# First-norm row factors multiplied in behind the products for the first pair of blocks, and the second pair's gates one block product later

## The chip, the cores and the metric

The kernel runs on one NeuronCore of one Trainium2 chip. Its time is device microseconds of one execution. TensorE (PE) multiplies matrices into PSUM; VectorE (DVE), ScalarE (ACT) and GpSimd (POOL) work on SBUF and, the first two, on PSUM; SyncE (SP) and GpSimd issue most DMA transfers. Each engine takes its instructions in order.

## What is computed

One layer of a decoder trunk on x, 2048 rows of 1024 fp32 values:

```python
h = rmsnorm(x, norm_mix_g)                   # x * rsqrt(mean(x*x) + eps) * g
u = h @ w_in                                 # 3*512 + 2*1024 columns
gate_b, gate_c, v, x_r, g = split(u)
y_conv = gate_b * causal_dwconv(gate_c * v, conv_w)       # 3 taps
xr = causal_dwconv(x_r, rnn_conv_w) + rnn_conv_b          # 4 taps
r, i = sigmoid(blockdiag(xr, w_a) + b_a), sigmoid(blockdiag(xr, w_x) + b_x)
log_a = -8 * r * softplus(-lru_lambda); a = exp(log_a)
s[t] = a[t] * s[t-1] + sqrt(-expm1(2*log_a)) * (i * xr)[t]
y_rnn = s * gelu(g)
x = x + concat[rmsnorm(y_conv), rmsnorm(y_rnn)] @ w_out
x = x + square(relu(rmsnorm(x) @ w_mlp_in)) @ w_mlp_out
out = rmsnorm(x)
```

The first line has a factor for each row (1 over its root mean square) and a gain for each of the 1024 columns. A row factor commutes with the product by w_in, a gain does not.

## The kernel before

**Tiles.** Channels lie on the 128 partitions and rows on the free axis, so h is read transposed, from a transposed x in HBM (x_t, tiles xT). The 2048 rows are four blocks of 512, worked on in two pairs. A weight or an h value is kept as two rounded parts, hi and lo, and a product of 128 x 128 by 512 is three matmuls, hi by hi, hi by lo, lo by hi. round_off (L165 to L167) makes the parts: ScalarE copies to hi, VectorE subtracts for lo.

**First pair, mixers_plain.** The columns of w_in are worked in groups of 256, in the order x0 g0 x1 g1 x2 g2 x3 g3 c0 v0 c1 v1 b0 b1. A group on one block is 48 matmuls into one PSUM tile of two banks (ps_x, ps_g and so on; start_x for x0 on block 0), and there are four such tiles. For each pair of x and g, the two units u0 and u1 (class Lru, 128 channels each) do the recurrence: conv makes xr and its parts xr_hi and xr_lo; gate sends 12 matmuls into two PSUM tiles called psri, followed by four sigmoids that make r and gi; scan makes the coefficients, with tanh, exponential and square root on ScalarE, and runs the recurrence; out multiplies by gelu(g) into gi and adds the square to acc. u1's gate comes behind the next pair's x on block 0.

**Weights.** A unit of w_in is two tiles of 512 KB called raw, split into w_hi and w_lo. Some halves are spilled to HBM (d_ws) for the second pair. keep_sums makes four sums of raw weights (weight_sums, L638 to L641) and stores them (d_wk), also for the second pair. Tiles come from pools with a fixed number of slots, so a tile waits for the last user of its slot.

**The start.** The rows of block 0 are loaded in two halves (x), squared on ScalarE and summed; norm_rows makes the row factors; spread makes diagonals of them (L361) and multiplies by ones on TensorE (bc, L368), so that a factor stands on all partitions; scale_rows (L373) multiplies xT by it and the gain; the result is split to h_hi and h_lo. WARM matmuls of ones by ones (L385, L388) fill TensorE ahead. Block 1 goes the same way in prepare_second, between g0 and x0 on it, with its rows in xq.

**Second pair, mixers_blocks.** Two blocks and two halves of the contraction make 2 x 2 products, done with seven block products of 24 matmuls each (L778), in the order 1, 2, 6, 5, 7, 3, 4. The gates, scans and outs of the group before are placed behind the block products by the table STEPS: step 0 is u0's gate and u1's conv, 1 u0's scan, 2 u1's gate and u0's out, 3 u1's scan, 4 u1's out. The first group has a row of its own.

**Order.** Outside parts that stand as written (manual_schedule, around x0 on block 0), a scheduler of the framework moves instructions on each engine within what data, slots and issue_after (hold these behind a named instruction) allow. So the order in the code is not quite that on the engines.

Of the kernel before, what the change touches and what calls it, by code (L numbers as in the profile page):

```python
# [14 lines left out]
P = 128  # L15
SEQ = 2048
D = 1024
KD = D // P
# [11 lines left out]
WARM = 6  # L30
# [9 lines left out]
STEPS = {1: (0,), 2: (1,), 6: (2,), 5: (3,), 7: (4,)}  # L40
# [19 lines left out]
def block_kernel(  # L60
# [60 lines left out]
    def load(dst, src):  # L121
        nc.sync.dma_start(dst, src)
# [65 lines left out]
    def split_unit(u):  # L188
        if u >= len(units) or u in splits:
            return  # L190
        load_unit(u)
        rs = raws.pop(u)
        n = units[u][3]
        pairs = [split_new(r, wtile, "w") for r in rs]
# [80 lines left out]
    def load_xt_part(b, th):  # L275
        for q in range(2):
            r = temp("xT", (P, 4, 256))
            c0 = b * TB + th * 256
            src = x_t[q * 512 : q * 512 + 512, c0 : c0 + 256]
            xtt[b, q, th] = r  # L280
            load(r, src.rearrange("(k p) s -> p k s", p=P))

# [18 lines left out]
    load_x(0, (0,))  # L301
    load(prm, params)
    load_xt_part(0, 0)
    load_x(0, (1,))
    load_unit(0)
    load_xt_part(0, 1)
# [36 lines left out]
    def squares(b, ts):  # L343
        s2 = [small("s2_%d" % i)[:, : len(ts)] for i in range(2)]
        for i in range(2):
            for k, t in enumerate(ts):
                xv = x_half(b, t, i)
                nc.scalar.activation(xv, xv, AF.Square, accum_out=s2[i][:, k : k + 1])
        return s2

# [23 lines left out]

    start_x = psum("start_x")
    with tc.manual_schedule(
        engines={nc.scalar.engine, nc.vector.engine, nc.tensor.engine}
    ):
        h0 = (
            hp.tile([P, KD, TB], F32R, tag="h", name="h_hi"),  # L380
            hp.tile([P, KD, TB], F32R, tag="h", name="h_lo"),
        )
        rs = norm_rows(squares(0, (0, 1)), 2)
        for _ in range(WARM):
            nc.tensor.matmul(start_x[:, 0, :P], ones, ones, start=True, stop=True)  # L385
        bc = spread(rs, 2)
        for _ in range(WARM):
            nc.tensor.matmul(start_x[:, 0, :P], ones, ones, start=True, stop=True)  # L388
        sq = squares(0, (2, 3))

        def first(th, q, ns=range(3)):
            for n in ns:
                a, b = ((0, 0), (0, 1), (1, 0))[n]
                for j in range(2):
                    for k in range(4):
                        nc.tensor.matmul(
                            start_x[:, j, 256 * th : 256 * th + 256],
                            w_first[a][q][:, k, j * P : (j + 1) * P],
                            h0[b][:, 4 * q + k, 256 * th : 256 * th + 256],
                            start=q == 0 and n == 0 and k == 0,  # L400
                            stop=q == 1 and n == 2 and k == 3,
                        )

        for th in range(2):
            sl = slice(256 * th, 256 * th + 256)
            r = [xtt[0, q, th] for q in range(2)]
            hi = [h0[0][:, 4 * q : 4 * q + 4, sl] for q in range(2)]
            lo = [h0[1][:, 4 * q : 4 * q + 4, sl] for q in range(2)]
            scale_rows(r[0], 0, bc, 4)
            nc.scalar.copy(hi[0], r[0])  # L410
            scale_rows(r[1], 4, bc, 4)
            if th == 0:
                rs = norm_rows(sq, 2)
                w_first = take("x0", ahead=0)
                first(0, 0, (0,))
                bc = spread(rs, 2)
            nc.scalar.copy(hi[1], r[1])
            for q in range(2):
                V.tensor_tensor(lo[q], r[q], hi[q].bitcast(F32), SUB)
            first(th, 0, range(1 - th, 3))  # L420
            first(th, 1)
        split_unit(1)
# [12 lines left out]
    V.tensor_scalar(l_neg, lam, -1.0, 0.0, MUL, MAX)  # L435
    V.scalar_tensor_tensor(l_abs, l_neg, 2.0, lam, MUL, ADD)
    nc.scalar.activation(l_u, l_abs, AF.Exp, scale=-1.0)
    V.tensor_scalar(l_d, l_u, 2.0, None, ADD)
    V.reciprocal(l_d, l_d)
    V.tensor_mul(l_w, l_u, l_d)  # L440
    V.tensor_mul(l_w2, l_w, l_w)
    V.tensor_scalar(l_s, l_w2, 2.0 / 15, 2.0 / 13, MUL, ADD)
    for n in (11, 9, 7, 5, 3, 1):
        V.tensor_mul(l_s, l_s, l_w2)
        V.tensor_scalar(l_s, l_s, 2.0 / n, None, ADD)
    V.tensor_mul(l_s, l_s, l_w)
    V.tensor_add(l_s, l_s, l_neg)
    V.tensor_scalar(sp4, l_s, -4.0, None, MUL)
    V.tensor_scalar(sp8, l_s, -8.0, None, MUL)
# [8 lines left out]

    class Rows:

        def __init__(self, b, rs):
            self.b = b
            self.rs = rs
            self.s2 = [small("s2_%d" % i) for i in range(2)]

        def part(self, n):
            th, dh = n // 2, n % 2
            r = temp("xq")
            load(r, x_rows(self.b, th, dh))
            for k in range(2):  # L470
                c = 2 * th + k
                nc.scalar.activation(
                    r[:, k], r[:, k], AF.Square, accum_out=self.s2[dh][:, c : c + 1]
                )

        def factors(self):
            norm_rows(self.s2, NT, self.rs)

        def spread(self, bc):
            nc.scalar.copy(bc, spread(self.rs, NT))  # L480
# [172 lines left out]
    def mixers_plain(h):  # L653
# [3 lines left out]
        nxt = [Rows(2 + k, rs_next[:, k, :]) for k in range(2)]  # L657

# [6 lines left out]
        for pr in range(4):  # L665
            u0, u1 = Lru(2 * pr), Lru(2 * pr + 1)
            xin = new_xin(pr)
            g = wide("g")

            def drain_x(blk, ps):  # L670
                nc.scalar.copy(block(xin, blk, 3), ps)
# [24 lines left out]
            u1.conv(xin)  # L696
            both("g%d" % pr, drain_g, (1,), wg)
            u0.gate(gw)
            u0.scan()
            p0, p1, gp_ = u0, u1, g  # L700
            keep_sums(pr)
            for n in range(2):
                nxt[pr // 2].part(2 * (pr % 2) + n)
            if pr % 2:
                nxt[pr // 2].factors()
        us = []
        for pr in range(2):
            gc = wide("gc")
            cv = new_cv(pr)
            wc = both("c%d" % pr, lambda blk, ps: nc.scalar.copy(block(gc, blk), ps), (0,))  # L710
            if pr == 0:
                p1.gate(gw)
            both("c%d" % pr, lambda blk, ps: nc.scalar.copy(block(gc, blk), ps), (1,), wc)
# [10 lines left out]
            us.append(conv_short(pr, cv))  # L724
            keep_sums(4 + pr)
# [140 lines left out]
    def mixers_blocks(H, more):  # L866
# [7 lines left out]
        for n in range(-FETCHW, len(seq)):  # L874
# [327 lines left out]
    def prepare_second():  # L1202
        rows = Rows(1, small("rs_x"))
        for n in range(4):
            rows.part(n)
        load_xt(1)
        rows.factors()
        bc = temp("bcs", (P, TB))
        rows.spread(bc)
        his, los = [], []  # L1210
        for q in range(4):
            r = xtt[1, q]
            scale_rows(r, 2 * q, bc, 2)
            hi, lo = split_new(r, temp, "h1")
            his.append(hi)
            los.append(lo)
        h[1] = lambda k: (his[k // 2][:, k % 2, :], los[k // 2][:, k % 2, :])

# [224 lines left out]
```

## Time and profile before

| | us |
|---|---|
| median of 3 runs | 2199.39 (2197.33 to 2199.86) |
| the profiled execution | 2200.14 |
| its span, first to last instruction | 2198.3 |
| TensorE busy in the span | 2138.3 |
| VectorE busy | 1481.1 |
| ScalarE busy | 994.7 |

About 1.9 us of an execution lie outside the span. A row of the view by windows gives the busy time of each engine in one stretch, with its instructions in brackets, and at the end the clock that TensorE was granted (1.00 is full), the share of time that the DMA engines were busy, and GB/s. A row of the view of waits names an operation, what it waited for, the total, the number of times and the longest. TensorE's matmuls overlap, so the distance of two starts and not the length is what one costs.

### The profile page before, as it was taken

What the parts mean: (1) busy time and instruction counts of PE and PEld (TensorE: products, weight loads), DVE (VectorE), ACT (ScalarE), POOL (GpSimd) and SP (SyncE); (2) the same over time, 40 slices, a digit from 0 to 9 for tenths busy, and PEclk for the clock granted to TensorE, in tenths of its full rate; (3) what the DMA queues carried; (4) which work ended last, traced back from release to release, by engine and by line L of the source; (5) the groups of instructions that cost most, each with busy time, mean ns of one, the idle gap of its engine ahead of it and who ended that gap; (6) DMA issues with size and microseconds to landing.
All of it is one profiled execution on the core that took longest, in us unless ns stands there. A gap on an engine that the chain in (4) does not pass through costs nothing.

```text
span 2198.3 us, 25153 instructions
## 1 busy us (share of the span) xinstructions
PE 2138.3 (97%) x9514; PEld 1755.2 (80%) x9514; DVE 1481.1 (67%) x1739; ACT 994.7 (45%) x1238; POOL 165.9 (8%) x288
## 2 busy tenths in 40 slices
PE   6999999999999999999998999999999999999998
PEld 5777787888887888888887777878878888888886
DVE  6688864669877786577764778466887565654456
ACT  5688712435323335454535786244533333433333
POOL 0111110000111110000131121000000000000000
PEclk9999999999999999999999999999999999999999
DMA  9645565431786789799673554655134444876431
GB/s 335 215 165 187 210 223 183 156 138 53 283 300 248 292 310 403 273 385 341 236 255 118 167 182 154 224 177 182 49 124 183 150 166 153 320 290 234 163 141 77
DMA packets 179593, 464.14 MB, mean 211 GB/s; under 512 B 15376, under 2 KB 64528, under 8 KB 179472
## 3 DMA queue, kind: packets, MB, share of 16 engines
q1 hardware_dynamic: 146416, 346.12, 43.9%
q0 software_dynamic: 30176, 106.97, 13.1%
q10 hardware_dynamic: 2880, 9.44, 1.2%
q8 instruction: 75, 1.23, 0.2%
q14 instruction: 46, 0.38, 0.1%
HBM read 308.33 MB, written 154.14 MB: 210 GB/s over the span
## 4 chain that ended last, share of the span: by engine, by line
PE 78%; DVE 12%; ACT 4%; DMA 3%; issue 3%; SPq 0%; POOL 0%; DVEq 0%; ACTq 0%; POOLq 0%
PE dn L1064 28%; PE up L778 21%; PE po L241 11%; PE in L778 10%; PE ps_b L222 2%; PE ps_v L222 2%; PE ps_c L222 2%; DMA w<-in_w_mlp_out_dram 1%; DVE w_lo L167 1%; DVE xr L496 1%; DVE xr L540 1%; DMA xq<-in_x_dram 1%; PE psri L510 1%; PE ps_x L222 1%; DVE H L167 1%
## 5 line engine op out<-in xcount | busy, mean ns | idle before, releaser
L778 PE MATMUL up<-H,w_hi 128*128 128x512 f32 x1792 | 554.4, 391 | 4.2 <-DVE snap L970 3.4
L167 DVE TENSOR_TENSOR w_lo<-w,w_hi 128x1024 fp32r<-128x1024 f32 x208 | 253.0, 1220 | 224.1 <-issue 119.3
L778 PEld LDWEIGHTS up<-H,w_hi 128*128 128x128 f32 x1792 | 336.9, 188 | 75.3 <-ACT H L166 4.2
L778 PE MATMUL up<-H,w_lo 128*128 128x512 f32 x896 | 349.9, 391 | 3.8 <-DVE w_lo L167 3.8
L1064 PE MATMUL dn<-w_hi,z_hi 128*128 128x512 f32 x896 | 349.2, 390 | 1.6 <-DVE x L1381 1.6
L1064 PE MATMUL dn<-w_lo,z_hi 128*128 128x512 f32 x896 | 348.9, 389 | 0.0
L1064 PE MATMUL dn<-w_hi,z_lo 128*128 128x512 f32 x896 | 348.6, 389 | 0.0
L166 ACT CAST w_hi<-w 128x1024 fp32r<-128x1024 f32 x208 | 216.4, 1049 | 138.7 <-PE dn L1064 90.3
L778 PE MATMUL in<-H,wr 128*128 128x512 f32 x888 | 206.1, 393 | 1.4 <-ACT g L800 1.4
L778 PEld LDWEIGHTS up<-H,w_lo 128*128 128x128 f32 x896 | 168.8, 188 | 39.3 <-DVE w_lo L167 4.3
L778 PEld LDWEIGHTS in<-H,wr 128*128 128x128 f32 x888 | 167.4, 189 | 39.6 <-ACT g L800 1.8
L1064 PEld LDWEIGHTS dn<-w_hi,z_hi 128*128 128x128 f32 x896 | 168.2, 188 | 37.2 <-DVE x L1381 2.4
L1064 PEld LDWEIGHTS dn<-w_lo,z_hi 128*128 128x128 f32 x896 | 168.2, 188 | 35.8 <-DVE w_lo L167 0.8
L1064 PEld LDWEIGHTS dn<-w_hi,z_lo 128*128 128x128 f32 x896 | 168.2, 188 | 35.2
L166 ACT CAST z_hi<-z 128x1024 fp32r<-128x1024 f32 x112 | 117.7, 1051 | 168.4 <-PE dn L1064 155.9
L167 DVE TENSOR_TENSOR z_lo<-z,z_hi 128x1024 fp32r<-128x1024 f32 x112 | 136.7, 1221 | 79.4 <-issue 45.6
L167 DVE TENSOR_TENSOR w_lo<-raw,w_hi 128x1024 fp32r<-128x1024 f32 x76 | 92.8, 1222 | 111.2 <-ACT w_hi L166 57.5
L166 ACT CAST w_hi<-raw 128x1024 fp32r<-128x1024 f32 x76 | 79.6, 1053 | 153.1 <-PE po L241 85.0
L957 ACT COPY snap<-up 128x1024 f32<-128x1024 f32 x48 | 48.7, 1014 | 185.1 <-PE up L778 181.2
L241 PE MATMUL po<-w_hi,y_hi 128*128 128x512 f32 x384 | 119.2, 392 | 3.5 <-ACT y_hi L624 3.5
L241 PE MATMUL po<-w_hi,y_lo 128*128 128x512 f32 x384 | 118.5, 390 | 0.2
L241 PE MATMUL po<-w_lo,y_hi 128*128 128x512 f32 x384 | 118.5, 390 | 0.0
(247 smaller groups left out, 3113.2 us busy)
## 6 DMA issues: line engine op xcount, KB each, us to landing
z<-d_z SPq DMA_DIRECT2D x112, 512.0 KB, 7.3
w<-in_w_mlp_out_dram SPq DMA_DIRECT2D x80, 512.0 KB, 5.7
wr<-d_ws POOLq DMA_DIRECT2D x74, 512.0 KB, 5.1
w<-in_w_mlp_in_dram SPq DMA_DIRECT2D x64, 512.0 KB, 4.7
d_z<-snap SPq DMA_DIRECT2D x64, 512.0 KB, 3.0
w<-d_w SPq DMA_DIRECT2D x64, 512.0 KB, 4.8
raw<-in_w_out_dram SPq DMA_DIRECT2D x48, 512.0 KB, 3.7
d_z<-z SPq DMA_DIRECT2D x48, 512.0 KB, 3.0
```

Source lines behind the costliest of these rows:

```text
L166: nc.scalar.copy(hi, src)
L167: latest[0] = V.tensor_tensor(lo, src, hi.bitcast(F32), SUB).ins
L222: nc.tensor.matmul(ps[:, j, :], ws[k // 4][:, k % 4, j * P : (j + 1) * P], hs, start=k == 0 and i == 0, stop=k == KD - 1 and i == len(pl) - 1,
L241: nc.tensor.matmul(ps[:, half, :], ys[:, j, t * P : (t + 1) * P], ws[j][:, 0, half * 512 : (half + 1) * 512], start=first and i == 0, stop ...
L496: V.scalar_tensor_tensor(xr, xin[:, j, k : k + 2 * TB], par("rnn_conv_w", 8 * k + c), xr, MUL, ADD)
L510: nc.tensor.matmul(ps[e][:, blk, :], ws[head[e], j, :], xs[head[e], blk * TB : blk * TB + TB], start=i == 0, stop=i == len(pl) - 1,)
L540: V.tensor_tensor_scan(v, r, gi, state[:, c, :], MUL, ADD)
L778: nc.tensor.matmul(ps[:, j, :], ws[:, k, j * P : (j + 1) * P], hs(k), start=i in (1, 2, 5) and k == 0 and n == 0, stop=k == 3 and n == len ...
L957: nc.scalar.copy(t, ps)
L1064: nc.tensor.matmul(ps[t // 2][:, t % 2, :], zs[:, p, t * P : (t + 1) * P], ws[:, p, :], start=i in (1, 2, 5) and a == 0 and p == 0 and n == 0,
```

## The change

For the first pair of blocks, x^T times the gain goes into the products, and the factors R (one row of [128, 2, 512], spread as before) are multiplied in as the products leave PSUM:

- gained makes hi (ScalarE, a copy with a scale) and lo (VectorE) from xT and the gain, in halves of 512 columns.
- The drains of x and g are VectorE products by R (x was a ScalarE copy, g a ScalarE gelu; the gelu now follows in place). The drain of c is a product by R squared (it was a ScalarE copy), v as before; the output u of the short convolution is multiplied by R.
- The start loads x^T and w_in first, in quarters; the row tiles of both blocks follow as xq. x0 and g0 on block 0 and x0 on block 1 can run ahead of their factors. x0 on block 0 is 48 matmuls of 512 columns in place of 96 of 256. WARM goes from 6 twice to 24 once.
- The softplus of lru_lambda, keep_sums, and six weight spills are held behind other work; those spills move from SP to POOL.
- STEPS puts each step of the second pair one block product later, and for its first group u0's gate stays and u1's comes one product later.

```diff
-WARM = 6
+WARM = 24
-STEPS = {1: (0,), 2: (1,), 6: (2,), 5: (3,), 7: (4,)}
+STEPS = {2: (0,), 6: (1,), 5: (2,), 7: (3,), 3: (4,)}
...
-                kept[n, i] = [spill_r("ws", t, nc.sync if u < 2 else nc.gpsimd) for t in pairs[half]]
+                if u < 2:
+                    held.append((n, i, pairs[half]))
+                else:
+                    kept[n, i] = [spill_r("ws", t, nc.gpsimd) for t in pairs[half]]
...
+    for q in range(4):
+        load_xt(0, (q,))
+        piece = slice(2 * (q % 2), 2 * (q % 2) + 2)
+        load(raw_first[q // 2][:, piece], units[0][1][q // 2][:, piece])
     load_unit(1)
...
+    firsts = [Rows(k, small("rs_x")) for k in range(2)]
+    load_xt(1)
+    firsts[0].fetch()
+    firsts[1].fetch()
+
+    def gained(r, q, hi, lo):
+        for j in range(2):
+            g = par("norm_mix_g", 2 * q + j)
+            a = nc.scalar.activation(hi[:, j, :], r[:, j, :], AF.Copy, scale=g)
+            V.scalar_tensor_tensor(
+                lo[:, j, :], r[:, j, :], g, hi[:, j, :].bitcast(F32), MUL, SUB
+            )
+        return a.ins
...
             def drain_x(blk, ps):
-                nc.scalar.copy(block(xin, blk, 3), ps)
+                V.tensor_mul(block(xin, blk, 3), ps, over(R, blk))
 
             def drain_g(blk, ps):
-                nc.scalar.activation(block(g, blk), ps, AF.Gelu_apprx_tanh)
+                V.tensor_mul(block(g, blk), ps, over(R, blk))
+                nc.scalar.activation(block(g, blk), block(g, blk), AF.Gelu_apprx_tanh)
 
             if pr == 0:
+                pss = []
+                wg = both("g0", lambda blk, ps: pss.append(ps), (0,))
+                with tc.issue_after(prepare_second()):
+                    for n in range(4):
+                        firsts[0].part(n)
+                firsts[0].factors()
+                firsts[0].spread(R[:, 0, :])
                 drain_x(0, start_x)
-                wg = both("g0", drain_g, (0,))
-                prepare_second()
-                both("x0", drain_x, (1,), w_first)
+                drain_g(0, pss[0])
+                for n in range(4):
+                    firsts[1].part(n)
+                both("x0", lambda blk, ps: pss.append(ps), (1,), w_first)
+                firsts[1].factors()
+                firsts[1].spread(R[:, 1, :])
+                seen = nc.gpsimd.tensor_copy(warm, R[:, 1, 0:1]).ins
+                with tc.issue_after(seen):
+                    for n, i, pair in held:
+                        kept[n, i] = [spill_r("ws", t, nc.gpsimd) for t in pair]
+                drain_x(1, pss[1])
...
             u1.conv(xin)
+            late = latest[0]
             both("g%d" % pr, drain_g, (1,), wg)
...
-            keep_sums(pr)
+            with tc.issue_after(late):
+                keep_sums(pr)
...
+        R2 = temp("R2")
+        nc.scalar.activation(R2, R, AF.Square)
...
+            def drain_c(blk, ps):
+                V.tensor_mul(block(gc, blk), ps, over(R2, blk))
...
+            for blk in range(2):
+                V.tensor_mul(block(us[pr], blk), block(us[pr], blk), over(R, blk))
...
-                for step in ({6: (0,), 5: (1, 2), 7: (3, 4)} if s == 1 else STEPS).get(i, ()):
+                for step in ({6: (0,), 5: (1,), 7: (2,), 3: (3,), 4: (4,)} if s == 1 else STEPS).get(i, ()):
```

The queue of transfers at the start, on SP. Before (xT is x^T of block 0, raw a half of a weight unit, x a part of the rows):

```order
L122 DMA x<-in_x_dram 128x2x512 x2
L122 DMA prm<-in_params_dram 128x96
L122 DMA xT<-in_x_t_dram 128x4x256 x2
L122 DMA x<-in_x_dram 128x2x512 x2
L122 DMA raw<-in_w_in_dram 128x4x256 x2
L122 DMA xT<-in_x_t_dram 128x4x256 x2
L122 DMA raw<-in_w_in_dram 128x4x256 x2
L131 DMA d_ws<-w_hi 128x1024
```

And with the change; the pair of xT and raw behind prm stands there four times:

```order
L122 DMA prm<-in_params_dram 128x96
L122 DMA xT<-in_x_t_dram 128x2x512
L122 DMA raw<-in_w_in_dram 128x2x256
...
L122 DMA raw<-in_w_in_dram 128x4x256 x2
L122 DMA xT<-in_x_t_dram 128x2x512 x4
L122 DMA xq<-in_x_dram 128x2x512 x8
```

The rows of x have gone from the first place to behind ten tiles of x^T and weights, and the spills (d_ws) have left the queue.

TensorE at the first gate, right behind g0 on block 1. Before, u0's gate (psri) is followed by x1 on block 0, all 48 matmuls of it, and then u1's gate:

```order
L510 MATMUL psri<-xr_hi,gate 128x512 x2
L510 MATMUL psri<-xr_lo,gate 128x512 x2
L510 MATMUL psri<-xr_hi,gate 128x512 x4
L510 MATMUL psri<-xr_lo,gate 128x512 x2
L510 MATMUL psri<-xr_hi,gate 128x512 x2
L222 MATMUL ps_x<-h_hi,w_hi 128x512
L222 MATMUL ps_x<-h_lo,w_hi 128x512
L222 MATMUL ps_x<-h_hi,w_lo 128x512
```

With the change:

```order
L498 MATMUL psri<-xr_hi,gate 128x512 x2
L498 MATMUL psri<-xr_lo,gate 128x512 x2
L498 MATMUL psri<-xr_hi,gate 128x512 x4
L498 MATMUL psri<-xr_lo,gate 128x512 x2
L498 MATMUL psri<-xr_hi,gate 128x512 x2
L229 MATMUL ps_x<-h_hi,w_hi 128x512
L229 MATMUL ps_x<-h_lo,w_hi 128x512
L498 MATMUL psri<-xr_hi,gate 128x512
L498 MATMUL psri<-xr_lo,gate 128x512
L498 MATMUL psri<-xr_hi,gate 128x512 x2
```

u1's gate has moved ahead: two matmuls of x1 stand between the gates, and the other 94 behind them.

ScalarE in the second pair, from the sigmoids of the second group's u0 to the rounding for its u1 (the activation that writes xr from r is the tanh, the one that writes r the exponential, the one that writes xr from gi the squaring in out of the unit before). Before:

```order
L521 ACT_TABLE_LOAD
L521 ACTIVATE r<-psri,prm 64x1024
L550 ACTIVATE xr<-gi 128x1024
L126 DMA d_y<-gi 128x1024
L524 ACTIVATE gi<-psri,prm 64x1024
L521 ACTIVATE r<-psri,prm 64x1024
L524 ACTIVATE gi<-psri,prm 64x1024
L533 ACTIVATE xr<-r,sp_335 128x1024
L534 ACT_TABLE_LOAD
L534 ACTIVATE r<-r,sp_336 128x1024
L166 CAST xr_hi<-xr 128x1024
```

With the change:

```order
L509 ACTIVATE r<-psri,prm 64x1024
L512 ACTIVATE gi<-psri,prm 64x1024
L509 ACTIVATE r<-psri,prm 64x1024
L512 ACTIVATE gi<-psri,prm 64x1024
L538 ACTIVATE xr<-gi 128x1024
L126 DMA d_y<-gi 128x1024
L815 COPY xr_in<-in 128x2x512
L521 ACTIVATE xr<-r,sp_253 128x1024
L522 ACT_TABLE_LOAD
L522 ACTIVATE r<-r,sp_254 128x1024
L166 CAST xr_hi<-xr 128x1024
```

The squaring has moved behind the sigmoids, and a copy out of PSUM stands ahead of the tanh. On TensorE u1's gate comes 48 matmuls after u0's in these groups before and after the change; in the first group it was 24 and is 48.

More of the change, by code (lines that the diff above doesn't have):

```diff
@@ L192, in split_unit, with note_split @@
         rs = raws.pop(u)
+        note_split(u, rs, [split_new(r, wtile, "w") for r in rs])
+    held = []
+    def note_split(u, rs, pairs):
         n = units[u][3]
-        pairs = [split_new(r, wtile, "w") for r in rs]
         if n is not None:
@@ L373, in scale_rows, with __init__, fetch, part @@
             V.scalar_tensor_tensor(r[:, k, :], r[:, k, :], par("norm_mix_g", k0 + k), bc, MUL, MUL)
+    class Rows:
+        def __init__(self, b, rs):
+            self.b = b
+            self.rs = rs
+            self.s2 = [small("s2_%d" % i) for i in range(2)]
+            self.raw = {}
+        def fetch(self, ns=range(4)):
+            for n in ns:
+                self.raw[n] = temp("xq")
+                load(self.raw[n], x_rows(self.b, n // 2, n % 2))
+        def part(self, n):
+            th, dh = n // 2, n % 2
+            if n not in self.raw:
+                self.fetch((n,))
+            r = self.raw.pop(n)
+            for k in range(2):
+                c = 2 * th + k
+                nc.scalar.activation(
+                    r[:, k], r[:, k], AF.Square, accum_out=self.s2[dh][:, c : c + 1]
+                )
+        def factors(self):
+            norm_rows(self.s2, NT, self.rs)
+        def spread(self, bc):
+            nc.scalar.copy(bc, spread(self.rs, NT))
+    firsts = [Rows(k, small("rs_x")) for k in range(2)]
[8 more added lines that the diff above has]
+                lo[:, j, :], r[:, j, :], g, hi[:, j, :].bitcast(F32), MUL, SUB
+            )
+        return a.ins
     start_x = psum("start_x")
@@ L378, in block_kernel @@
     ):
+        for _ in range(WARM):
+            nc.tensor.matmul(start_x[:, 0, :P], ones, ones, start=True, stop=True)
         h0 = (
@@ L382, in block_kernel @@
         )
[L383 to L421, printed above, removed]
@@ L422, in block_kernel @@
-        split_unit(1)
+        pairs = [(wtile("w_hi", WSHAPE, F32R), wtile("w_lo", WSHAPE, F32R)) for _ in range(2)]
+        for q in range(4):
+            sl = slice(2 * q, 2 * q + 2)
+            piece = slice(2 * (q % 2), 2 * (q % 2) + 2)
+            gained(xtt[0, q], q, h0[0][:, sl], h0[1][:, sl])
+            whi, wlo = (t[:, piece] for t in pairs[q // 2])
+            round_off(whi, raw_first[q // 2][:, piece], wlo)
+        note_split(0, raw_first, pairs)
+        w_first = splits.pop(0)
@@ L424, in block_kernel @@
+        cursor[0] = 1
+        for k in range(KD):
+            for j in range(2):
+                mm_cols(start_x, w_first, lambda k: (h0[0][:, k, :], h0[1][:, k, :]), j, (k,))
     lam = prm[:, off["lru_lambda"] : off["lru_lambda"] + 8]
@@ L434, in block_kernel @@
     sp8 = cp.tile(L8, F32, name="sp8")
[L435 to L449, printed above, removed]
+    with tc.issue_after(latest[0]):
+        V.tensor_scalar(l_neg, lam, -1.0, 0.0, MUL, MAX)
+        V.scalar_tensor_tensor(l_abs, l_neg, 2.0, lam, MUL, ADD)
+        nc.scalar.activation(l_u, l_abs, AF.Exp, scale=-1.0)
+        V.tensor_scalar(l_d, l_u, 2.0, None, ADD)
+        V.reciprocal(l_d, l_d)
+        V.tensor_mul(l_w, l_u, l_d)
+        V.tensor_mul(l_w2, l_w, l_w)
+        V.tensor_scalar(l_s, l_w2, 2.0 / 15, 2.0 / 13, MUL, ADD)
+        for n in (11, 9, 7, 5, 3, 1):
+            V.tensor_mul(l_s, l_s, l_w2)
+            V.tensor_scalar(l_s, l_s, 2.0 / n, None, ADD)
+        V.tensor_mul(l_s, l_s, l_w)
+        V.tensor_add(l_s, l_s, l_neg)
+        V.tensor_scalar(sp4, l_s, -4.0, None, MUL)
+        V.tensor_scalar(sp8, l_s, -8.0, None, MUL)
     halo = cp.tile([P, NLRU, 3], F32, name="halo")
@@ L457, in block_kernel @@
     nc.gpsimd.memset(state, 0.0)
[L459 to L480, printed above, removed]
     class Lru:
@@ L657, in mixers_plain, with over @@
         nxt = [Rows(2 + k, rs_next[:, k, :]) for k in range(2)]
+        R = temp("R")
+        def over(t, blk):
+            return t[:, blk : blk + 1, :].broadcast_to([P, 2, TB])
         def both(nm, drain, blks=range(2), w=None):
@@ L1202, in prepare_second @@
     def prepare_second():
[L1203 to L1209, printed above, removed]
         his, los = [], []
         for q in range(4):
-            r = xtt[1, q]
-            scale_rows(r, 2 * q, bc, 2)
-            hi, lo = split_new(r, temp, "h1")
+            hi, lo = (temp("h1", dt=F32R) for _ in range(2))
+            last = gained(xtt[1, q], q, hi, lo)
             his.append(hi)
```

25 lines of the change are left out of this document (4 added, 21 removed).

## The prediction

> **What bounds the kernel now.** I read the page first, then busy time by stage, then TensorE's waits, then timelines where the waits lie.
>
> ```profile
> span 2198.3 us, 25153 instructions
> PE 2138.3 (97%) x9514; PEld 1755.2 (80%) x9514; DVE 1481.1 (67%) x1739; ACT 994.7 (45%) x1238; POOL 165.9 (8%) x288
> ```
>
> TensorE is the bound: 60.0 us of the span are all it idles, and slow clocks come on top. No edit here takes a full product away, so a gain has to come out of idle time and half-speed time. The next view (busy time by window, with granted clock, DMA share and GB/s at the end) says where these lie.
>
> ```profile
> core 0: us, PE busy (x) PEld busy (x) DVE busy (x) ACT busy (x) POOL busy (x), PEclk, DMA share, GB/s
> 0.00:20.00 20.00, 7.25 (x28) 6.48 (x29) 9.51 (x48) 12.60 (x27) 1.65 (x11) 1.00 0.92 324
> 20.00:50.00 30.00, 26.44 (x148) 22.78 (x146) 21.14 (x37) 15.02 (x29) 0.00 (x0) 1.00 0.97 354
> 50.00:56.80 6.80, 6.23 (x14) 4.45 (x15) 6.80 (x9) 3.74 (x5) 1.07 (x2) 0.50 0.70 264
> 124.00:172.20 48.20, 47.50 (x216) 37.93 (x214) 38.60 (x41) 40.35 (x45) 8.49 (x10) 1.00 0.54 191
> 172.20:224.20 52.00, 49.59 (x217) 39.31 (x216) 42.08 (x38) 43.73 (x48) 8.42 (x10) 0.97 0.53 193
> 1190.00:1196.80 6.80, 3.88 (x14) 2.34 (x15) 4.34 (x5) 4.80 (x7) 0.00 (x0) 0.50 0.01 4
> 1234.40:1241.20 6.80, 6.09 (x19) 4.08 (x20) 5.61 (x6) 5.60 (x6) 0.53 (x1) 0.50 0.27 95
> 1326.50:1333.30 6.80, 5.77 (x18) 3.86 (x19) 5.77 (x6) 6.75 (x7) 1.06 (x2) 0.50 0.17 48
> ```
>
> The first 20 us hold 7.25 us of TensorE work while DMA is nearly full, and a clock of 0.50 comes four times for 6.8 us. TensorE's waits, the first two up to 420 us and the others from 1125 to 1410 us (total, times, longest):
>
> ```profile
> PE bc L368 <- DVE diag L361: 10.1, 2, 9.4
> PE ps_x L222 <- ACT h_hi L166: 3.3, 1, 3.3
> ...
> PE psri L510 <- ACT xr_hi L166: 11.1, 3, 5.5
> PE psri L510 <- DVE xr_lo L167: 2.3, 4, 0.7
> ```
>
> The start waits for row factors (9.4 us); the second pair for rounded gate inputs, once 5.5 us and twice about 2.8 us ((11.1 - 5.5) / 2). Each of these brings a half-clock stretch.
>
> **The start.** TensorE's timeline (start, length, line, operation, idle before it):
>
> ```profile
> 1.14 2.93 PE L385 MATMUL start_x<-ones 128*128 128x128 f32 x12 [1.14 <-POOL ones L252]
> 13.49 1.22 PE L368 MATMUL bc<-diag,ones 128*128 128x256 f32 x2 [9.42 <-DVE diag L361]
> 19.47 0.80 PE L396 MATMUL start_x<-h_hi,w_hi 128*128 128x256 f32 x2 [2.20 <-ACT w_hi L166]
> 35.22 0.40 PE L222 MATMUL ps_g<-h_hi,w_hi 128*128 128x512 f32 x1
> ...
> 75.10 0.39 PE L222 MATMUL ps_g<-h_lo,w_hi 128*128 128x512 f32 x1
> 75.33 0.39 PE L222 MATMUL ps_g<-h_hi,w_lo 128*128 128x512 f32 x1
> 75.65 0.50 PE L510 MATMUL psri<-xr_hi,gate 64*128 64x512 f32 x2
> ...
> 101.91 0.39 PE L222 MATMUL ps_g<-h_hi,w_hi 128*128 128x512 f32 x1
> ```
>
> Products start 0.227 us apart (75.10 to 75.33), so 48 of them, one group on one block, take 10.9 us. The first four groups end at 75.65, and x1 on both blocks at 101.91.
>
> After the change x0 needs only x^T, a weight piece and the gain. A quarter of the contraction needs 768 KB; at 324 GB/s, counted from 2 us (an estimate of when data begins to flow), it lands near 4.5 us and the fourth near 12, one each 2.4 us, and TensorE takes 2.7 for each. Rounding adds some 3 us. The warm-up ends later than that: 12 recorded passes last 2.93 us, 0.244 each; 48 of them would end at 12.9 us if all stayed cold, and near 7 us at half that from the first pass. I take 9. So x0 on block 0 ends at 9 + 10.9 = 19.9, g0 at 30.8. The factors are due there. Their four row tiles come behind 12 tiles of 512 KB: 8.4 MB in all, at 340 GB/s landed by 27 us; two squares of the last tile, a table load, the root and the diagonals take about 4 us more (prices in the next rows; the small ones estimated at 0.2), so the spread waits 0 to 1 us. With 0.9 us for each spread (an estimate below the cold 1.22), x0 on block 1 ends at 42.8, g0 at **54.6**: 21.0 us earlier than 75.65.
>
> Not all of it stays. By the order shown above the second unit's gate now stands two products behind the first's, while both convolutions can begin only after the second spread. Prices, by groups of VectorE and ScalarE in the stretch of 124 to 172.2 us (busy in all, ns of one, idle before), and then one drain out of PSUM on VectorE from a later stage:
>
> ```profile
> L496 DVE SCALAR_TENSOR_TENSOR xr<-xr_in,prm,xr 128x1024 f32<-128x1024 f32 x6 | 7.7, 1275 | 0.0
> L167 DVE TENSOR_TENSOR w_lo<-raw,w_hi 128x1024 fp32r<-128x1024 f32 x4 | 4.9, 1220 | 7.3 <-DMA d_wk<-raw 7.3
> L492 DVE TENSOR_SCALAR xr<-xr_in,prm 128x1024 f32<-128x1024 f32 x1 | 0.8, 807 | 0.0
> L521 ACT ACTIVATE r<-psri,prm 64x1024 f32<-64x1024 f32 x4 | 4.4, 1112 | 0.1
> L521 ACT ACT_TABLE_LOAD x3 | 3.8, 1283 | 0.1
> L472 ACT ACTIVATE xq<-xq 128x512 f32<-128x512 f32 x4 | 2.5, 620 | 1.9 <-DMA xq<-in_x_dram 1.9
> L166 ACT CAST xr_hi<-xr 128x1024 fp32r<-128x1024 f32 x2 | 2.1, 1056 | 0.2
> L671 ACT COPY xr_in<-ps_x 128x1024 f32<-128x1024 f32 x2 | 2.0, 1014 | 0.0
> L722 DVE TENSOR_TENSOR cv<-ps_v,gc x4: 1216/1216/1225, 265.7 to 317.6; 128x1024 f32<-128x1024 f32 x4
> ```
>
> From the end of x0, A = 42.8: spread and copy 1.5, drain 1.2, convolution 0.8 + 3 x 1.28 = 4.6, rounding 1.05 and remainder 1.2: the first gate is ready at 52.4, in time. The second unit: again 4.6, the gating drain 1.2 between, 1.05, 1.2, so A + 17.8 = 60.6. Its PSUM comes free after four 1.11 us sigmoids and a table load behind that rounding, 62 to 65, and the lower halves of x1's weights stand behind four raw sums (4.9, priced like w_lo) and their stores, near 67. TensorE wanted the gate at 54.6 + 1.66 + 0.5 = 56.8. It idles 6 to 8 us in pieces and then runs a stretch at 0.50: 9 to 11 us lost. x1 ends at 58.4 + 94 x 0.227 + 10.5 = 90 rather than 101.9, **12 us** won; 8 with every piece at its worst, 16 if the sums slip past the remainders.
>
> **First pair, later groups.** Each pair's VectorE work grows by four drains of 1.22 us, 4.9 (ScalarE loses two copies of 1.01): 38.6 + 4.9 = 43.5 of the 47.5 us that TensorE works in that stretch. That still fits beneath TensorE; the cover is 4 us a pair, and the 7.3 us that VectorE sits on one store fills most of it. PSUM slots are now freed by VectorE in its queue, with two gates and remainders behind the drain, and TensorE asks for the slot about 12 us later. Moving keep_sums behind the remainders helps. I take +1 us, from -4 (one stall with its half clock more) to +5 (what the pair of 172.2 to 224.2 us loses against the one before, and half a stall more). R squared, four products on u in the convolution groups, and POOL's spills lie where VectorE has room; the spill must only be past before the second weights' buffers are asked for, 20 us later. I cost them at nothing; a late spill would stop a lower half and so TensorE by 3 us.
>
> **Second pair.** ScalarE before the worst wait:
>
> ```profile
> 1180.52 1.28 ACT L521 ACT_TABLE_LOAD   x1
> 1181.81 1.11 ACT L521 ACTIVATE r<-psri,prm 64x1024 f32<-64x1024 f32 x1
> ...
> 1185.18 1.11 ACT L524 ACTIVATE gi<-psri,prm 64x1024 f32<-64x1024 f32 x1
> 1186.75 1.01 ACT L800 COPY g<-in 128x1024 f32<-128x1024 f32 x1 [0.45 <-PE in L778]
> 1187.65 1.15 ACT L533 ACTIVATE xr<-r,sp 128x1024 f32<-128x1024 f32 x1
> 1188.82 1.28 ACT L534 ACT_TABLE_LOAD   x1
> 1190.12 1.15 ACT L534 ACTIVATE r<-r,sp 128x1024 f32<-128x1024 f32 x1
> 1191.17 1.03 ACT L166 CAST xr_hi<-xr 128x1024 fp32r<-128x1024 f32 x1
> ```
>
> The rounding that the second gate needs is queued behind the first unit's sigmoids, tanh and exponential and ends at 1192.2, 12.8 us after that gate began at 1179.4. TensorE asked one block product later (24 x 0.227 = 5.4 us, plus 1.66 for the gate). With a second product between, it asks 5.4 us later: the 5.5 us wait falls to about 0.1, and to 1 with the remainder behind it. Half clock cost there (30 - 14) x 0.227 = 3.6 us against the full-clock count of the 6.8 us window, partly this same wait; with 3.3 us of wait ahead of the window, 6.9 in all; 6 won. The two 2.8 us waits cost about 0 + 11 x 0.227 = 2.5 and 12 x 0.227 = 2.7 in their windows and 2.8 ahead of them, 5.3 and 5.5. In their groups both gates move together and stay two products apart, and a chain of the unit before still goes ahead of them in both queues. But the squaring that stood between the sigmoids now stands after them. I leave the first in place and let the second go with a chance of one in two and a bit: 6 + 0.5 x 5.5 + 1 = **10**, from 4 to 17 (all three gone).
>
> At the two 2.8 us idles the clock fell to 0.50. The Trainium skill (TensorE: Matmul & The Clock Gate, HAM oscillation) names gaps above about 3.4 us as what throttles; the trace does not agree, 2.8 was enough. By the page these waits would be worth only their own 2.8, and the sum 1 us less.
>
> **Sum.** 12 + 1 + 10 = 23 us from the profiled execution's 2200.14: 2177. The runs' median is 0.75 below it, within their spread of 2.5.
>
> **Rivals.**
> *VectorE becomes the bound of the first pair.* For it: 43.5 us of work plus 7.3 of store wait is 50.8 a pair, over 48.2. A PSUM drain takes 1.216 us there against 1.014 on ScalarE. Against: much of that wait is slack that shrinks when more work is ahead of it. 2.6 x 3 = 8 us, with two half-clock stretches of 2.6: 13 us, 2190. The Trainium skill (Perfetto Trace Analysis, Optimizing Scalar/DVE Operations) advises to give work to ScalarE where VectorE is saturated; this change goes the other way.
> *The later gates bring nothing*, because the delayed chain meets the next group's gate: 2177 + 10 = 2187.
> *Both of these*: 2200, no change.
> *Slower*: with its PSUM slots freed in VectorE's queue, each of the eight gates of the first pair finds its remainder over 2.8 us late, and each such wait also halves the clock: 8 x 5.4 = 43 us, less the 5 lost now: 2215. It decides once VectorE trails by more than 2.8 us at six of eight gates. Against: the start alone leaves room of 12 us.
>
> **Chances.** The forecast 0.63, VectorE as the bound 0.13, later gates in vain 0.14, both 0.05, slower 0.05. A measurement of this kernel tells about 0.2%, 4.4 us, from no change. Faster: 0.63 + 0.13 + 0.14 = 0.90; same 0.05; slower 0.05. The forecast's own terms reach from 2200 - 38 = 2162 (16, 5, 17) to 2200 - 8 = 2192 (8, -4, 4), which covers the two nearest rivals: 2162 to 2192.
>
> **What would show it.** The profile after should have no wait for a diagonal over 1.5 us, x0's products from about 9 us, g0's end on block 1 near 54.6 and a gap of 6 to 8 us right behind it; the waits of psri for xr_hi should fall from 11.1 to 3 to 6, with the 5.5 gone. Wrong would be: a start held beyond 12 us by DMA, waits of products for drains in the first pair, or three half-clock stretches still after 1180 us.

## The result

The change runs in 2184.37 us (median of 4 runs, 2183.31 to 2186.98) against 2199.62 (2197.33 to 2202.31) for the kernel before in the same series: the ratio is 0.9932, 95% interval 0.9915 to 0.9949, 15 us. The profiled execution has a span of 2181.5 us, 16.8 below the 2198.3 of before. The page after (busy time, share and instructions):

```profile
span 2181.5 us, 25122 instructions
PE 2135.1 (98%) x9488; PEld 1754.3 (80%) x9488; DVE 1499.2 (69%) x1742; ACT 986.1 (45%) x1236; POOL 169.1 (8%) x295
```

TensorE idles 46.4 us instead of 60.0. Its waits after, up to 420 us and behind that (those that belong to the change or to its surroundings; up and dn are the two products of the MLP, by w_mlp_in and w_mlp_out):

```profile
PE psri L498 <- ACT gi L512: 6.8, 2, 5.0
PE psri L498 <- ACT xr_hi L166: 2.8, 1, 2.8
...
PE bc L359 <- DVE diag L352: 1.0, 1, 1.0
PE psri L498 <- DVE xr_lo L167: 0.8, 1, 0.8
...
PE up L796 <- DVE w_lo L167: 4.8, 1, 4.8
PE psri L498 <- DVE xr_lo L167: 3.7, 4, 1.0
PE psri L498 <- ACT xr_hi L166: 3.4, 3, 2.2
...
PE in L796 <- DVE w_lo L167: 2.9, 1, 2.9
...
PE dn L1082 <- DVE w_lo L167: 0.9, 1, 0.9
```

The 9.4 us wait for the first diagonal is gone and a wait of 1.0 has come; the second pair's waits for xr_hi fell from 11.1 to 3.4. psri's waits for gi grew from 2.1 to 6.8, one for a lower weight half near 1348 us grew from 1.0 to 2.9, and new are one of 2.8 for xr_hi at the first gates and one of 0.9 in dn. TensorE's timeline after, at the start, at the first gate and at the end of x1:

```profile
1.14 8.53 PE L415 MATMUL start_x<-ones 128*128 128x128 f32 x48 [1.14 <-POOL ones L259]
9.42 0.47 PE L229 MATMUL start_x<-h_hi,w_hi 128*128 128x512 f32 x1
...
56.17 0.51 PE L498 MATMUL psri<-xr_hi,gate 64*128 64x512 f32 x2
...
91.25 0.39 PE L229 MATMUL ps_g<-h_hi,w_hi 128*128 128x512 f32 x1
```

The first gate stands at 56.17 rather than 75.65, 19.5 us earlier, and x1 has ended at 91.25 rather than 101.91, 10.7 us earlier. Nearly half of what the start won was lost within 35 us. Busy time by window shows it, and the last three rows show the slow stretches of the second pair:

```profile
0.00:20.00 20.00, 18.86 (x95) 17.05 (x96) 11.86 (x24) 14.13 (x22) 1.65 (x11) 1.00 0.92 321
20.00:50.00 30.00, 29.02 (x125) 23.04 (x124) 18.11 (x51) 18.61 (x47) 0.92 (x3) 1.00 0.54 200
55.90:62.70 6.80, 3.22 (x18) 1.68 (x16) 5.60 (x6) 3.51 (x4) 0.00 (x0) 0.94 0.00 0
62.70:72.50 9.80, 9.80 (x23) 6.75 (x24) 8.03 (x7) 8.09 (x8) 2.44 (x5) 0.52 0.80 266
224.00:232.00 8.00, 3.42 (x12) 2.32 (x13) 7.90 (x7) 7.76 (x7) 0.00 (x0) 0.61 0.78 292
1225.70:1229.10 3.40, 3.18 (x12) 2.16 (x13) 2.24 (x4) 2.48 (x3) 0.53 (x1) 0.52 0.65 230
1314.60:1318.00 3.40, 3.30 (x12) 2.27 (x13) 3.40 (x5) 3.12 (x4) 0.46 (x1) 0.50 0.31 108
1348.70:1352.00 3.30, 3.30 (x9) 2.65 (x8) 2.13 (x3) 2.13 (x3) 1.78 (x3) 0.50 0.52 146
```

Three readings of the traces follow the time through the kernel, in us: the start of the first b0 product (the end of the x, g, c and v groups), of the second pair's block products, and of the first product by w_out behind them.

| kernel | b0 | block products | w_out | span |
|---|---|---|---|---|
| before | 318.15 | 1124.90 | 1433.22 | 2198.3 |
| change | 309.95 | 1117.50 | 1416.76 | 2181.5 |
| gained over before | 8.2 | 7.4 | 16.5 | 16.8 |

So the first pair keeps 8.2 us of 10.7, 0.8 goes between, and the second pair wins 9.1. The 0.8 us are lost in dn: its first product starts at 809.9 rather than 818.2, 8.3 us earlier, and the new wait of 0.9 us comes after that. up waits longer for w_lo, 4.8 us rather than 3.8, but loses nothing by its end.

### The profile page after: what moved, and what is told of

It is laid out like the page before. It is cut to its first block, busy times and chain, and to the rows that moved or that the text cites. A ratio compares the mean times of both kernels' runs of the same rounds, so it can differ in the third digit from the quotient of the medians.

```text
span 2181.5 us, 25122 instructions
## 1 busy us (share of the span) xinstructions
PE 2135.1 (98%) x9488; PEld 1754.3 (80%) x9488; DVE 1499.2 (69%) x1742; ACT 986.1 (45%) x1236; POOL 169.1 (8%) x295
## 4 chain that ended last, share of the span: by engine, by line
PE 75%; DVE 13%; ACT 4%; issue 4%; DMA 4%; SPq 0%; POOL 0%; DVEq 0%; ACTq 0%; POOLq 0%
PE dn L1082 28%; PE up L796 19%; PE po L248 11%; PE in L796 7%; DMA w<-in_w_mlp_out_dram 2%; PE ps_b L229 2%; PE ps_v L229 2%; PE ps_x L229 2%; PE ps_c L229 2%; DVE xr L484 1%; DVE w_lo L167 1%; DVE xr L528 1%; DMA d_w<-w 1%; PE psri L498 1%; DVE xr_lo L167 1%
## 5 line engine op out<-in xcount | busy, mean ns | idle before, releaser
L166 ACT CAST w_hi<-raw 128x1024 fp32r<-128x1024 f32 (+1 forms) x78 | 80.0, 1031 | 166.7 <-PE po L248 85.2
L167 DVE TENSOR_TENSOR w_lo<-raw,w_hi 128x1024 fp32r<-128x1024 f32 (+1 forms) x78 | 93.1, 1194 | 85.1 <-ACT w_hi L166 58.6
```

The source lines that it names most:

```text
L166: nc.scalar.copy(hi, src)
L167: latest[0] = V.tensor_tensor(lo, src, hi.bitcast(F32), SUB).ins
```

## The experiments

The theory after the prediction: two independent gains; the start wins nearly 20 us, and loses half of it since lower weight halves stand behind the raw sums; the second pair's gates win by their distance. The rivals: the gains lean on each other, and VectorE, not an order, bounds the first pair.

**The two parts apart.** One kernel has only the new table rows, one all but them:

```diff
-STEPS = {1: (0,), 2: (1,), 6: (2,), 5: (3,), 7: (4,)}
+STEPS = {2: (0,), 6: (1,), 5: (2,), 7: (3,), 3: (4,)}
-{6: (0,), 5: (1, 2), 7: (3, 4)} if s == 1
+{6: (0,), 5: (1,), 7: (2,), 3: (3,), 4: (4,)} if s == 1
```

> The kernel before with the new places of the second pair's gates alone. Theory (two independent gains, of about 8 us from the start and the first pair and about 9 from these gates): 9 us faster than before, 2190; the waits of psri for xr_hi after 1100 us fall from 11.1 to about 3.5 us. Rival (the delayed steps only pay because the changed start leaves the second pair's queues in another state): no change, 2199. It tells how much of the 15 us these two lines bring.

> The change with the old places of the second pair's gates. Theory (independent gains): 7 to 8 us faster than before, 2192, with the 5.5 us wait back. Rival (the start is everything and the later gates bring nothing): 15 us faster, 2184. If it and the run with the gates alone add up to 15 us, nothing is shared between the parts.

Measured: the gates alone 0.9953 (0.9939 to 0.9966), 10 us; the start alone 0.9966 (0.9953 to 0.9979), 7.5 us. The sum, 18 us, agrees with the 15 of both within the intervals. In the traces the gates alone bring w_out forward by 9.7 us (1423.53 against 1433.22) with b0 where it was (317.71), and the start alone brings b0 to 309.90 as in the change, with the waits for xr_hi back at 11.1 us. The runs show no dependence of the parts on each other, to within some 5 us of their intervals.

**The first gates.** The four raw sums of the first groups were put ahead of the second spread:

```diff
                 for n in range(4):
                     firsts[1].part(n)
+                keep_sums(0)
```

(and for this pair no longer behind `late`).

> The change with the first pair's four raw sums put ahead of the second spread, not behind the remainders; the scheduler then leaves x1 on block 0 between the two first gates, 48 products and not 2. Theory (19.5 us are won by the end of g0 and 9 are lost again because x1's lower weights stand behind the sums and their stores, so that the second gate has nothing ahead of it): the 9 us stay won, x1 ends near 82 rather than 91.2, the whole 7 to 9 us faster than the change, 2176. Rival (VectorE is late as such, by the drains and convolutions that can begin only after the second spread): the wait moves to x1's weights or to xr_lo, less than 3 us are won.

It took 0.9958 (0.9943 to 0.9973), some 6 us more than the change, neither of the two. (The execution in its trace took 2187.60, less than the run's median of 2193.38, so the trace does not show all of that loss.) From the first gate to the end of x1 there was no wait left: 68.10 to 93.40, 25.3 us where the change takes 35.1. But TensorE had waited 11.4 us for a diagonal of the first block's factors. VectorE's timeline of that run says why:

```profile
33.70 0.29 DVE L352 TENSOR_SCALAR diag<-ident,rs_x 128x128 f32<-128x128 f32 x1
40.27 1.22 DVE L167 TENSOR_TENSOR w_lo<-raw,w_hi 128x1024 fp32r<-128x1024 f32 x1 [6.28 <-DMA d_wk<-raw]
41.41 0.67 DVE L352 TENSOR_SCALAR diag<-ident,rs_x 128x128 f32<-128x128 f32 x3
```

A remainder that needs the slot of a sum still being stored stands between the first diagonal and the other three. The loss at the gates was the sums' place, as the theory said; the place chosen here moved the wait up the queue. So the sums went right behind the second spread's diagonals:

```diff
                 firsts[1].spread(R[:, 1, :])
+                with tc.issue_after(last_diag[0]):
+                    keep_sums(0)
```

> The change with the first pair's four raw sums right behind the diagonals of the second spread, where VectorE sat idle for 6.3 us. The run with the sums ahead of everything lost 11.4 us at the spread, since a lower weight half that waits for the sums' stores then stood between the diagonals; here it cannot. Theory (the sums' place makes the 9 us loss at the first two gates): psri waits less than 1 us up to 100 us, x1 ends at 82 to 86, 5 to 8 us faster than the change, 2178. Rival (VectorE is late as such): a lower half that waits for its store now holds the drain of x0, and the first gate is late by 3 us or more, with a half-clock stretch; under 3 us won.

0.9907 (0.9893 to 0.9920), 5 us faster than the change. Its waits between 50 and 100 us, beside the end of x1:

```profile
PE psri L500 <- ACT xr_hi L166: 1.5, 1, 1.5
PE psri L500 <- DVE xr_lo L167: 0.8, 1, 0.8
...
85.63 0.39 PE L229 MATMUL ps_g<-h_hi,w_hi 128*128 128x512 f32 x1
```

x1 ended at 85.6, 5.6 us earlier, as the theory had it; the remaining wait is the rival's, for here too VectorE waits on a store, 3.93 us, ahead of x0's drain. Yet b0 starts only 3.2 us earlier, 306.77: 2.4 of the 5.6 us are lost again in between, at the third pair's second gate. There psri waits 3.9 us for gi and a half-clock stretch of 3.4 us follows, from 172.1; the change waits 1.8 us at that gate, 0.6 for ps_x, and has no such stretch. At the fourth pair's second gate the wait is 2.1 rather than 5.0 us.

**The waits for gi.** In the change ScalarE had, around the fourth pair's first gate, which TensorE finished at 212.1:

```profile
220.29 1.05 ACT L166 CAST xr_hi<-xr 128x1024 fp32r<-128x1024 f32 x1 [2.49 <-DVE xr L484]
221.36 1.28 ACT L509 ACT_TABLE_LOAD   x1
222.66 1.11 ACT L509 ACTIVATE r<-psri,prm 64x1024 f32<-64x1024 f32 x1
223.77 1.28 ACT L667 ACT_TABLE_LOAD   x1
225.06 1.06 ACT L667 ACTIVATE g<-g 128x1024 f32<-128x1024 f32 x1
226.13 1.28 ACT L512 ACT_TABLE_LOAD   x1
227.42 1.11 ACT L512 ACTIVATE gi<-psri,prm 64x1024 f32<-64x1024 f32 x1
```

A gelu with a table load before and behind it lies between the sigmoids, and all of it behind a rounding that waits for VectorE's convolution. TensorE waits 5.0 us for the activation that writes gi at 227.42. In four other runs whose first pair is the same code, all of it or all but the warm-up (the start alone, and below the first group's row alone, the second gate later and 8 warm-up matmuls), that wait is 3.4 us, yet these activations start within 0.3 us of the times above and b0 within 0.1 us of 309.95: TensorE came to the gate later, after a half-clock stretch near 178 us that the change does not have. So ScalarE's row sets the time here. One edit moves the gelu:

```diff
             u0.gate(gw)
+            if pr == 3:
+                with tc.issue_after(u0.last):
+                    nc.scalar.activation(block(g, 1), block(g, 1), AF.Gelu_apprx_tanh)
```

> The change with one gelu, that of the fourth pair on block 1, put behind the four sigmoids of that pair's first gate instead of between them. Theory (the 5.0 us wait of the second gate for gi there comes from two table loads and a gelu of 1.06 us between the sigmoids, 3.6 us, since VectorE now drains g): the wait falls to about 1.4 us and its half-clock stretch goes, 4 to 6 us faster than the change, 2179. Rival (VectorE's load is the bound there): the wait goes over to another operand of the same gate or of c0, within 1.5 us of the change.

0.9909 (0.9895 to 0.9923), 5 us faster than the change. The waits between 80 and 320 us and the new row of sigmoids:

```profile
PE psri L498 <- ACT gi L512: 1.9, 1, 1.9
...
222.59 1.11 ACT L509 ACTIVATE r<-psri,prm 64x1024 f32<-64x1024 f32 x1
223.72 1.11 ACT L512 ACTIVATE gi<-psri,prm 64x1024 f32<-64x1024 f32 x1
```

The 5.0 us wait is gone; the 1.9 stands at the third pair's gate. b0 starts at 305.15, 4.8 us earlier. up then waits 6.0 us for w_lo near 660 us, 1.2 more than in the change, but the wait of dn is gone, and the block products start at 1112.8, still 4.7 us earlier.

> The sums between and the one gelu behind its sigmoids together, on the change. Theory (two stalls at two places with nothing in common): the sum of both, 5 to 8 and 3 to 5 us, 2174. Rival (time won early is taken by the next stall, as the fourth pair's was by the first's): no faster than the better one of the two.

With both edits the time was 0.9906 (0.9893 to 0.9920), no better than either; b0 at 305.39. The rival held: with the first gates early, TensorE waited 2.7 us for gi one pair before, with a half-clock stretch of 6.8 us, and 1.6 for a drain of c.

**VectorE's load.** One run was meant to tell load from order. The products by R on g were left out (so g lacks its row factor in this run):

```diff
             def drain_g(blk, ps):
-                V.tensor_mul(block(g, blk), ps, over(R, blk))
-                nc.scalar.activation(block(g, blk), block(g, blk), AF.Gelu_apprx_tanh)
+                nc.scalar.activation(block(g, blk), ps, AF.Gelu_apprx_tanh)
```

> The change without the factor on g: ScalarE's gelu reads PSUM as before and the products by R on g are left out, 2.44 us of VectorE work for each pair of blocks and group, 9.8 in all. It tells VectorE's load from VectorE's order. Theory (order sets the stalls, the load is covered): only what g's drain held goes, the 5.0 us wait of the fourth pair's second gate and its slow stretch, 3 to 6 us faster, and the first gates' wait for xr_hi falls by the 1.2 us of one drain. Rival (VectorE is the bound of the first pair): all its waits fall and 9 us or more are won.

0.9897 (0.9882 to 0.9913), 7.7 us faster than the change, between the two expectations, with 4.6 us of wait and a slow stretch at the first spread that the change does not have. From 80 us on TensorE waits for nothing up to b0 (303.87). Windows of the change and then of this run:

```profile
75.00:310.00 235.00, 227.56 (x1026) 184.85 (x1024) 194.15 (x180) 151.91 (x166) 34.05 (x48) 0.99 0.61 224
...
80.00:304.00 224.00, 223.97 (x1022) 182.53 (x1021) 187.24 (x174) 146.09 (x162) 31.93 (x48) 1.00 0.65 236
```

VectorE is busy 83% there in the one (194.15 of 235) and 84% in the other, and one stalls TensorE where the other does not. So its busy share does not tell the two apart; where VectorE is late, a rounding holds ScalarE's queue, with the sigmoids behind it. The edit changes order too, though: the gelu reads PSUM itself and no longer stands behind VectorE's drain. It therefore does not separate load from order, and by the intervals its gain of 7.7 us is clear of neither expectation. In the trace more went than the theory said, the 1.8 us wait at the third pair too.

**The second pair.** First the first group's row alone, with the general rows as before:

> The change with the new places for the first group's gates only; groups two to four stand as before, so that 72 and not 96 products lie between the first group's second gate and the second group's first. Theory (only the first group gains from the distance of its own two gates, 6 us; the others move together and give what the chain ahead of them gives): 5.5 us wait gone, the second group's wait longer than the 2.8 us of before by up to 5.4, the whole 3 to 6 us slower than the change, 2188. Rival (the general rows bring nothing): as the change, 2184.

0.9978 (0.9969 to 0.9987): 10 us slower than the change, more than expected, and no faster than with the rows of before (0.9966). Its waits behind 1160 us:

```profile
PE psri L498 <- ACT xr_hi L166: 10.9, 4, 3.7
PE psri L498 <- DVE xr_lo L167: 7.2, 7, 2.6
```

The 5.5 us wait is gone, but the second group's gates, now 24 products closer behind it, wait 0.9 and 3.7 us, the third's second gate 2.8 and the fourth's 3.4. The general rows, which I had credited with half of 5.5 us, are what keeps the first group's gain.

Then the second gate of groups two to four one product later still:

```diff
-STEPS = {2: (0,), 6: (1,), 5: (2,), 7: (3,), 3: (4,)}
+STEPS = {2: (0,), 6: (1,), 7: (2,), 3: (3,), 4: (4,)}
```

> The change with the second unit's gate of groups two to four one block product later still, so that 72 and not 48 products stand between the two gates of a group. Theory (there the wait for xr_hi is a distance that the change did not alter: 2.2, 1.0 and 0.3 us with half clock in the change): psri's waits for xr_hi go to 0.3 us or less after 1100 us, and 4 to 6 us are won, 2179. Rival (the chain behind the second gate then meets the next group's first gate, 96 and not 120 products on): waits there or at the outs, within 2 us of the change or slower.

0.9885 (0.9871 to 0.9898), 10 us faster than the change; w_out at 1407.42, 9.3 us earlier, of which 8.6 in the second pair. Its waits in the same stretch:

```profile
PE in L796 <- ACT w_hi L166: 2.2, 1, 2.2
PE in L796 <- DVE w_lo L167: 1.8, 2, 1.4
PE psri L498 <- DVE xr_lo L167: 0.9, 1, 0.9
```

No wait for xr_hi is left, and these rows sum to 4.9 us where the change waits 10.0. Of its three slow stretches one is left, near 1308. More was won than expected since the waits for xr_lo fell too, from 3.7 to 0.9, and the 2.9 us wait for w_lo near 1348 fell to 1.4 and lost its stretch. Against that stand new waits of 2.2 us for w_hi and 0.4 for w_lo near 1308, ahead of the stretch that is left. Why the waits for weights moved was not tried by itself.

**All together.** Sums between, later gates, and with or without the gelus of pairs two to four behind their sigmoids:

> The sums between, the gates of groups two to four one product later still, and the gelu on block 1 behind the first gate's sigmoids in pairs two to four. Theory (the stalls of the second pair lie 900 us behind those of the first, so these gains add): 10 us of the later gates and 5 of the sums below the change, 1 or 2 more for the gelus, 2168. Rival (gains taken by the next stall, as with sums and gelu together): 2174 or more.

> As the run with all three, without the gelus moved. Theory: 15 us below the change, 2170; the difference to the run with all three tells what the gelus' place is worth once the sums are moved: 0 to 2 us. Rival (the gelus matter by themselves): 4 us or more apart.

0.9878 (0.9863 to 0.9893) with the gelus, 0.9874 (0.9859 to 0.9889) without: 2174 us, 12 us below the change and 27 below the kernel before. Neither differs from the later gates alone (0.9885) by more than the intervals. The profiles differ by more, with spans of 2167.5 and 2172.5, b0 at 302.89 and 307.67 (309.89 with the later gates alone), but the runs do not show it. What the sums and the gelus bring on top of the later gates stays open.

**The warm-up.**

```diff
-WARM = 24
+WARM = 8
```

> The change with 8 warm-up matmuls (16 recorded passes) rather than 24 (48). The first parts of x0 are ready at 8.7 us and the warm-up ends at 9.4; the spread waits for its diagonal at 32.4. Theory (the factors' transfers and squares set the second block's start, not the warm-up): x0 starts at about 8 us, some of it at half clock, and what it wins or loses is taken up by the spread's wait; within 1.5 us of the change, 2184. Rival (the warm clock of the first products is what the warm-up buys): x0 and g0 run cold for 7 us or more, end after 33 us, and 2 to 4 us are lost.

0.9925 (0.9913 to 0.9938), as the change. The first rows:

```profile
1.14 3.78 PE L415 MATMUL start_x<-ones 128*128 128x128 f32 x16 [1.14 <-POOL ones L259]
7.71 0.79 PE L229 MATMUL start_x<-h_hi,w_hi 128*128 128x512 f32 x1 [2.79 <-ACT w_hi L166]
8.30 0.63 PE L229 MATMUL start_x<-h_lo,w_hi 128*128 128x512 f32 x1
8.73 0.63 PE L229 MATMUL start_x<-h_hi,w_lo 128*128 128x512 f32 x1
...
PE bc L359 <- DVE diag L352: 1.5, 1, 1.5
```

x0 starts 1.7 us earlier, has its next products 0.43 us apart until 10.4, and ends 0.35 us earlier; the spread then waits 1.5 us rather than 1.0 for its diagonal and stands at 32.6, as in the change (32.4). The view by windows reads a granted clock of 1.00 from 7.7 to 10.4 us, so at the start that column does not show products at half their rate (0.43 us apart where 0.227 is usual). The factors bound the start, not the warm-up.

## Why the prediction came out as it did

It said 2177 in a range of 2162 to 2192, from 23 us of gain; 15 were measured (16.8 between the profiled spans). Direction and parts were right; one term, the later groups of the first pair, was too large by 3.5 us, and smaller errors add up to the rest.

- **The start.** g0 was to end at 54.6 and ended at 56.2: x0 began at 9.42 (taken: 9), the spread waited 1.0 us (0 to 1). The rows stand behind twelve tiles of 512 KB, as the prediction counts, and not behind ten. Of the price of the warm-up, the bounds of 7 and 12.9 us held, but the term was idle: with 8 matmuls the spread stands where it stood. The step that sets it is the one behind, squares and diagonals. The prediction also lets the 9.4 us wait of the kernel before bring a half-clock stretch; its own row for 0 to 20 us reads 1.00 and shows none, though that column also missed the half rate of the products with 8 warm-up matmuls.
- **The first gates.** 9 to 11 us lost were forecast, by VectorE's queue row by row; 8.8 were lost, and 10.7 won at x1 for the 12 forecast. That this fits is partly luck: TensorE idled 3.6 us in two pieces and not 6 to 8, and the stretch at half clock was long, 10.2 us (granted 0.50 from 61.9 to 72.1). The mechanism, sums and stores ahead of x1's lower halves, was confirmed by the sums' other places: in the change the first of these halves is ready at 68.57 and used at 68.74, and the 35.1 us from g0's end to x1's end became 25.3 and 29.4. The second gate itself does not stand behind the sums (its remainder begins at 61.29, the first sum at 62.43); it is late by the convolutions, and the sums' place left only two products of x1 ahead of it, 48 with the sums moved. The steps up to that gate add to 17.6 us and not 17.8, on which nothing hangs.
- **The later groups of the first pair.** This step failed in size and in reason: +1 was forecast, -2.5 measured (10.7 at x1, 8.2 at b0), inside its bounds of -4 to +5. I had said that what is added fits beneath TensorE. It fits in sum and not in the queue: the late g drain put a gelu and two table loads between the sigmoids of the fourth pair, and a late convolution held the rounding ahead of them; 5.0 us at one gate in this trace, 3.4 in four others. Up to the end of g3 the change had still been gaining: its fourth pair's first gate stands at 210.4, 13.8 us before the 224.2 of the kernel before. The rival of VectorE as the bound is half right: not its busy share but its lag stalled TensorE, and leaving out g's products, 2.44 us of each pair and the gelu's wait with them, removed all waits behind 80 us. How much of that is load alone stays open.
- **The second pair.** 10 us forecast, 9.1 measured, from other parts than said, so that the sizes agree partly by luck; the 1 us behind 6 and 0.5 x 5.5 in that sum came from no row. The first wait went to 0 and some xr_lo, as forecast; the second did not stay at 2.8 but fell to 2.2, the third fell to 1.0, and their slow stretches from 6.8 to 3.4 us. A wait for w_lo grew from 1.0 to 2.9 us and took back part. So three half-clock stretches came after 1180 us all the same, at 1225.7, 1314.6 and 1348.7, which the prediction had named as a sign of being wrong; each lasts 3.4 us and not 6.8, and the third belongs to the weights. The general rows, priced at 2.75, were worth the whole gain: without them the first group's row brought nothing. What I had missed is the distance to the next group's gate: it is what a step gives up when only the one before it moves.
- **Between.** The wait of dn for w_lo, 0.9 us, is new in the change, and ranges from nothing to 2.1 us over these kernels; that of up, 3.8 before and 4.8 after, ranges from 3.7 to 6.0. The 0.8 us lost here was not in the sum.

The 3.5 us of the later groups, 1.3 at the start, 0.9 in the second pair and 0.8 between, less 0.3 won behind w_out, make the 6.2 us between 23 and the 16.8 of the profiles.

## What to carry to other kernels

When a stage starts earlier, price the next waits as if the stage's own engines had not moved: the work that was hidden behind the old wait (here raw sums, their stores and the lower halves that need their slots) now sets the time, and moving one such item up an in-order queue moves the wait with it unless nothing in front can stop. Free time on an engine is no cover by itself; what matters is which instruction stands behind the late one, on the other engines too. And where steps follow each other at fixed distances, a step that moves later must take its successors along.

## What was not expected of the hardware

Short idles were enough to halve TensorE's clock. Ahead of the stretch from 1314.6 to 1318.0 of the change, granted 0.50, TensorE had idled 0.99 and 0.96 us:

```profile
1313.23 0.50 PE L498 MATMUL psri<-xr_hi,gate 64*128 64x512 f32 x2 [0.99 <-ACT xr_hi L166]
1314.70 0.79 PE L498 MATMUL psri<-xr_lo,gate 64*128 64x512 f32 x2 [0.96 <-DVE xr_lo L167]
1315.29 1.05 PE L498 MATMUL psri<-xr_hi,gate 64*128 64x512 f32 x4
```

And the same idle of 1.76 us ahead of w_out's first product (po) left the clock alone in the change, and halved it in the run without R on g. The first two rows are of the change, the next two of that run:

```profile
366.42 0.74 PE L248 MATMUL po<-w_hi,y_hi 128*128 128x512 f32 x2 [1.76 <-ACT y_hi L612]
...
366.00:369.40 3.40, 2.90 (x11) 2.10 (x12) 3.40 (x5) 3.40 (x6) 0.00 (x0) 1.00 0.70 234
```

```profile
360.33 0.73 PE L248 MATMUL po<-w_hi,y_hi 128*128 128x512 f32 x2 [1.76 <-ACT y_hi L612]
...
362.00:365.30 3.30, 3.30 (x9) 2.61 (x8) 2.88 (x5) 1.35 (x3) 0.00 (x0) 0.50 0.90 277
```

So the length of one idle does not decide. Two equal idles with unequal outcomes are what one would see if the activity were counted in windows that run on by themselves, and the stretches come in 3.4 us, 6.8 and, at the first gates of the change, 10.2. The Trainium skill (TensorE: Matmul & The Clock Gate, Part 1: The HAM clock gate) describes such a free-running window of 3.4 us; the traces agree with that length, but not with its rule (there, HAM oscillation) that gaps above about 3.4 us are what throttles. How much of a window has to be idle these runs do not settle.
